# Eight of sixteen row blocks of x turned on VectorE, and the attention of quad 0 moved later, in a two-layer encoder step

## The chip, the cores and the metric

The kernel runs on one core of one Trainium2 chip. The metric is the device time of one execution in microseconds (us). It is an fp32 kernel: each product of the large projections is made of three fp32r matmuls on TensorE (PE). ACT and VectorE (DVE) split the weights, ACT and DVE also do the activations and the softmax, GpSimd (POOL) and SyncE (SP) mostly issue DMA transfers.

## The reference

One step of a two-layer encoder on 384 rows: 256 rows of a new stream ("prompt") and 8 running streams of 16 rows each ("sample"), with caches of 128 rows.

```python
DEPTH = 2; D_MODEL = 2048; SEQ = 256; DEC_BATCH = 8; DEC_SEQ = 16; PAST_LEN = 128
HEAD_DIM = 128; FOX_HEADS = 8; SB_HEADS = 8; C_WIDTH = 4096

def ab_project(h, w_in0, b_forget):
    p = jnp.einsum('bsd,dn->bsn', h, w_in0)        # q, k, v, gate of 8 + 8 heads, 8 forget logits
    ...

def fox_core(q, k, v, Fq, Fk, qpos, kpos):
    s = jnp.einsum('bqhd,bkhd->bhqk', q, k).astype(jnp.float32) * ATTN_SCALE
    s = s + (jnp.swapaxes(Fq, 1, 2)[..., :, None] - jnp.swapaxes(Fk, 1, 2)[..., None, :])
    s = jnp.where(kpos[None, :] <= qpos[:, None], s, -jnp.inf)
    p = jax.nn.softmax(s, axis=-1)
    return jnp.einsum('bhqk,bkhd->bqhd', p.astype(v.dtype), v)
```

Layer 0 is an RMSNorm, the projection above, forgetting attention (`fox_core`) for eight heads and stick-breaking attention for eight more, both gated, and an output projection with the residual added. Layer 1 is an RMSNorm, a projection to u, v and a gate, a spatial mix of the normalised v over 128 positions, and an output projection. A last RMSNorm follows. Outputs are the rows of both streams, and the new keys, values and forget logits.

## The kernel before

**Products.** A projection multiplies the 384 rows (three row tiles `tb` of 128) by 512 columns of a weight matrix, over 16 blocks `k` of 128 of the model's 2048 columns. The left operand is h, kept transposed as a high and a low half (`hhi`, `hlo`, tiles named `slot`). A weight tile of 128 rows by 512 columns comes over SP's queue (`raw`, five buffers). ACT casts it to its high half (`whi`, four buffers), DVE subtracts for its low half (`wlo`, four buffers), and `products` issues for two blocks at a time high x high (L100), high x low (L101) and low x high (L102): 18 matmuls of 128x512 for a pair of blocks. They are called products below. Their sums stand in a pool of four PSUM banks (`d`). All other matmuls share a second pool of four banks (`a`).

**Start.** The first projection (`first`, keys of heads 0 to 3) runs over the groups (0), (1), (2,3), ... (14,15) of blocks while x arrives in eight pieces of 256 columns over SP's queue (`load_piece`). For each block `x_transposes` turns three 128x128 tiles on TensorE (L219); ACT makes the high half of h out of PSUM, scaled by the norm's gain (L223, `slot<-a,gT`), and DVE the low half (L227). Group i+1's transposes and casts are issued between two parts of group i's products. The function `then` ties the instructions of an engine to the order in which they are written. After the last group the squares of x are summed for the norm (L271); the natural x in the `slot` tiles 94 to 97 is used for them too. The next projection (`values_first`: values of heads 0 to 3, in halves of 256 columns, with the forget logits) has weight tiles of 128x2x256 (L90).

**Quads.** After that, quads g of four heads each follow, g = 0 to 3, each with projections k, v, q and z (gate). The attention of a quad is done in two pairs of heads, and its steps are hooked into later projections: `at(g, what, kp, f)` calls f ahead of block pair kp of projection `what` of quad g. The steps of a pair are

- `scores`: the score matmuls of the new rows (L626, L627, L629) and of the cache (L632), softmax on DVE and ACT, and the writing of the weights to a DRAM tile `wd` over ACT's queue (L667). POOL then reads `wd` back in blocks of 32 by 32, four transfers `slot<-wd` (L492), so that DVE can turn them within the blocks.
- `attended`: two DVE transposes (L670) into the tiles `PT` of the two heads, the matmuls by the values (L678, L684 to L686) and by the cached values (L682), the gating on DVE, and the write of the result (`d<-gz`). The loads of the next heads' cached values follow (`vcache`, two buffers).
- `mix_split`, when both pairs are through: the gated result, read back over DRAM in blocks (`slot<-d`), is turned and split into halves for the output projection.

The order of an engine's instructions is set by a list scheduler that keeps the written order where `tc.issue_after` ties two instructions; each engine then runs its list in order and waits on semaphores.

**Norm gains.** `gains(1)` (L164, L165) turns the second norm's gains through one bank `a`. It stands ahead of the cumulative sums of the forget logits (L358 to L373), which take four banks.

Of the kernel before, what the change touches and what calls it, by code (L numbers as in the profile page):

```python
# [15 lines left out]
P = 128  # L16
# [16 lines left out]
def f32(ap):  # L33
    return ap.bitcast(F32)
# [3 lines left out]
def tile_hybrid_step(  # L38
# [27 lines left out]
    def bank():  # L66
        return psa.tile([P, 512], F32, tag="a", name=nm("a"))
# [36 lines left out]

    def dense_nat(w, k0, c0, his, los, nk=None, between=None, out=None, ks=None):


        nk = nk or len(his)
        out = out or [dbank() for _ in range(NT)]
        for kp in range(0, nk, 2) if ks is None else ks:  # L110
            behind = ()
            if between and kp in between:
                with tc.issue_after(splits[-1]), tc.issue_after(highs[-1]):
                    behind = between[kp]() or ()
            ws = [wunit(w[(k0 + k) * P:(k0 + k + 1) * P, c0:c0 + 512], 1, 512, behind=behind) for k in (kp, kp + 1)]
            products(out, his, los, ws, kp, range(NT), 0, nk - 1)
        return out
# [39 lines left out]
    with ExitStack() as l0:  # L157
# [29 lines left out]

        def load_raw():
            k = len(raws)
            raws.append(wload(w_in0[k * P:(k + 1) * P, 1024:1536], 1, 512))  # L190
# [24 lines left out]

        def x_transposes(k):
            b = bank()
            for tb in range(NT):
                then("PE", lambda: PE.transpose(b[:, tb * P:(tb + 1) * P], xs[k // 4][:, tb, k % 4 * P:k % 4 * P + P], ident))  # L219
            gcol = gT[:, k:k + 1]  # L220
            hi, lo = hhi[k // 4][:, k % 4, :], hlo[k // 4][:, k % 4, :]
            if k:
                high = then("ACT", lambda: S.activation(hi, b[:, :T], AF.Copy, scale=gcol))  # L223
            else:

                high = then("DVE", lambda: V.tensor_scalar(out=hi, in0=b[:, :T], scalar1=gcol, scalar2=None, op0=ALU.mult))
            return high, then("DVE", lambda: V.scalar_tensor_tensor(out=lo, in0=b[:, :T], scalar=gcol, in1=f32(hi), op0=ALU.mult, op1=ALU.subtract))  # L227
# [26 lines left out]
        for i, ks in enumerate(groups):  # L254
            then("PE", lambda: products(first, h0h, h0l, ws, ks[0], range(1), 0, KT - 1) if i else first_products(0))
            nxt = []
            if i + 1 < len(groups):
                if 1 <= i < 5:
                    load_piece(i + 3)
                while len(raws) < min(ks[-1] + 6, KT):  # L260
                    load_raw()
                nxt = [first_unit(k) for k in groups[i + 1]]
                done += [x_transposes(k) for k in groups[i + 1]]
# [79 lines left out]
        def forget(o):  # L343
# [12 lines left out]
            gains(1)  # L356
# [26 lines left out]
            V.tensor_copy(Fnat, b4[:, :24].rearrange("p (t h) -> p t h", h=8))  # L383
            nFT = lp.tile([8, 2 * T], F32, tag="PT", name="nFT")[:, :T]
# [81 lines left out]
        def quad(g):  # L466
# [11 lines left out]
            def scores(pair):  # L478
# [8 lines left out]
                for _ in range(2):  # L487
                    for j, hh in enumerate(pair):
                        own[hh].send(wd[j])
# [7 lines left out]
            def attended(pair):  # L497
                for j, hh in ((1, pair[1]), (0, pair[0])):
                    own[hh].send(own["blk", pair][:, j, :])
                for hh in pair:  # L500
                    next(own[hh])
# [9 lines left out]
            places = ((("z", 12), ("k", 2), ("k", 8), ("k", 12)), (("z", 12), ("v", 2), ("k", 2), ("k", 8)))[g > 0]  # L511
            at(g, "q", 2 if g == 0 else 14, lambda: turned("k"))
            at(g, "z", 12, lambda: turned("q"))
            for i, (what, kp) in enumerate(places):
                at(g + (what == "k"), what, kp, lambda i=i: (scores, attended)[i // 2](((0, 1), (2, 3))[i % 2]))
            at(g + 1, "q", (12, 8, 8, 8)[g], lambda: mix_split())
# [84 lines left out]
        def head(g, h, kT, values, qT, kc, vc, gate):  # L601
# [68 lines left out]
            V.transpose(out=PT, in_=blk)  # L670
            yield
# [320 lines left out]
```

## Time and profile before

| | us |
|---|---|
| three timed runs | 1812.33, 1812.5, 1813.67 (median 1812.5) |
| profiled execution, own time | 1815.39 |
| its span | 1813.7 |
| mean granted TensorE clock of the span | 0.995 |

The profile is one execution. Its span runs from the first to the last instruction, and the execution's own time lies 1.7 us above it. In a row of the timeline the two numbers ahead are the start and the length in us, `x8` counts instructions that follow one another, and the bracket holds the idle time of the engine just ahead and what ended it. Matmuls overlap, so that the distance from start to start is what one costs, not the length in its row. In a row of the windows stand busy time and count for PE, PEld (weight loads), DVE, ACT and POOL, then the granted clock, the share of the 16 DMA engines and GB/s. Names with a `q` (ACTq, POOLq, SPq) are the issues of DMA transfers on an engine's queue. The rows of ACT's largest wait read as follows.

```profile
ACT whi L84 <- PE d L102: 889.3, 379, 21.8
```

ACT waits 889.3 us in 379 places for TensorE to give back a `whi` buffer: the weight casts run ahead as far as four buffers let them, and TensorE paces them.

### The profile page before, as it was taken

To read this page: it belongs to the slowest core of one execution; us is meant where nothing else is said; L and a number is where in the kernel's file an instruction comes from. 1 tells how busy PE (TensorE), PEld (TensorE's weight loads), DVE (VectorE), ACT (ScalarE), POOL (GpSimd) and SP (SyncE) were. 2 spreads that over 40 slices of the span, in tenths; PEclk is the share of its full clock that TensorE was granted. 3 is DMA by queue.
4 is the path that set the end of the run, shared out by engine and by line. 5 is a ranking of instruction groups with operands and counts; after the bars stand their busy time and mean duration, and the time that the engine had idled before them with its cause. 6 is when DMAs were issued, how large, how long until landed. Compare 5 with 4: busy or idle time off the path is not lost. (4 is left out here: it accounts for less than half of the span.)

```text
span 1813.7 us, 24384 instructions
## 1 busy us (share of the span) xinstructions
PE 1788.8 (99%) x8575; PEld 1483.8 (82%) x8575; DVE 924.2 (51%) x1538; ACT 710.2 (39%) x1261; POOL 369.9 (20%) x544
## 2 busy tenths in 40 slices
PE   9999799999999999999999999999999999999998
PEld 8988588888888888888888888888888888888887
DVE  6337356458448455543433544554544563455366
ACT  5435236337337344433333333333333333333334
POOL 1515524313312202200300120320130210220020
PEclk9999899999999999999999999999999999999999
DMA  6868778878876877644444444454544554555553
GB/s 195 233 179 212 201 216 216 251 196 206 238 207 179 241 204 207 189 128 128 135 129 131 138 137 146 148 146 130 157 143 128 146 154 128 145 146 150 164 145 117
DMA packets 185771, 307.63 MB, mean 170 GB/s; under 512 B 22904, under 2 KB 63152, under 8 KB 185648
## 3 DMA queue, kind: packets, MB, share of 16 engines
q1 hardware_dynamic: 127696, 225.37, 42.1%
q0 software_dynamic: 25072, 63.53, 14.1%
q10 hardware_dynamic: 32880, 17.18, 3.2%
q8 instruction: 67, 1.10, 0.3%
q14 instruction: 56, 0.46, 0.1%
HBM read 269.23 MB, written 30.47 MB: 165 GB/s over the span
## 5 line engine op out<-in xcount | busy, mean ns | idle before, releaser
L86 DVE TENSOR_TENSOR wlo<-raw,whi 128x512 fp32r<-128x512 f32 x784 | 538.0, 695 | 745.1 <-ACT whi L84 744.9
L101 PE MATMUL d<-wlo,slot 128*128 128x512 f32 x2349 | 916.6, 391 | 0.2
L102 PE MATMUL d<-whi,slot 128*128 128x512 f32 x2349 | 912.0, 389 | 0.0
L84 ACT ACTIVATE whi<-raw 128x512 fp32r<-128x512 f32 x784 | 493.4, 631 | 944.9 <-PE d L102 889.3
L100 PE MATMUL d<-whi,slot 128*128 128x512 f32 x2349 | 822.9, 391 | 0.0
L100 PEld LDWEIGHTS d<-whi,slot 128*128 128x128 f32 x2349 | 440.9, 188 | 94.3 <-ACT whi L84 1.6
L101 PEld LDWEIGHTS d<-wlo,slot 128*128 128x128 f32 x2349 | 441.0, 188 | 91.7 <-DVE wlo L86 1.0
L102 PEld LDWEIGHTS d<-whi,slot 128*128 128x128 f32 x2349 | 441.0, 188 | 91.5
L126 POOL DMA_DIRECT2D gTt<-trn x128 | 78.0, 618 | 446.0 <-issue 263.9
L396 POOL DMA_DIRECT2D slot<-d x48 | 44.1, 924 | 145.9 <-DVE wlo L86 53.6
L492 POOL DMA_DIRECT2D slot<-wd x32 | 29.4, 924 | 103.4 <-DMA wd<-pr 34.6
L833 POOL DMA_DIRECT2D wr<-in_w_sp_dram x64 | 34.9, 553 | 26.2 <-DVE wT L837 25.1
L826 DVE TENSOR_TENSOR slot<-d,slot 128x512 f32<-128x512 f32 x48 | 32.0, 686 | 12.4 <-PE d L102 12.4
L783 POOL DMA_DIRECT2D slot<-in_sgu_ln_g_dram x8 | 4.5, 567 | 135.5 <-PE d L102 135.5
L455 POOL DMA_DIRECT2D kcache<-in_cache_sb_k_dram x32 | 24.9, 786 | 32.4 <-DVE KT L621 32.4
L455 POOL DMA_DIRECT2D kcache<-in_cache_fox_k_dram x32 | 25.0, 789 | 23.4 <-DVE KT L621 22.2
L709 POOL DMA_DIRECT2D blk<-h1d x12 | 11.0, 919 | 70.7 <-DMA h1d<-slot 60.4
L799 POOL DMA_DIRECT2D bcol<-in_b_sp_dram x1 | 1.2, 1176 | 116.1 <-DVE w L798 116.1
L862 PE MATMUL a<-vt,wT 128*128 128x256 f32 x96 | 24.5, 380 | 0.0
L777 POOL TENSOR_SCALAR rsv<-mvr 128x3 f32<-128x3 f32 x1 | 0.5, 540 | 113.0 <-DVE mvr L776 113.0
L774 DVE BATCH_NORM_STATS2 stats<-vt 128x6 f32<-128x512 f32 x24 | 16.3, 690 | 11.4 <-ACT vt L773 11.4
L849 DVE SCALAR_TENSOR_TENSOR gate<-d,rstd,gate 128x512 f32<-128x512 f32 x24 | 17.4, 748 | 7.3 <-PE d L102 7.3
(239 smaller groups left out, 1201.3 us busy)
## 6 DMA issues: line engine op xcount, KB each, us to landing
raw<-in_w_in_dram SPq DMA_DIRECT2D x640, 256.0 KB, 2.8
raw<-in_w_out_dram SPq DMA_DIRECT2D x189, 256.0 KB, 3.4
slot<-d POOLq DMA_DIRECT2D x48, 192.0 KB, 6.2
d<-slot ACTq DMA_DIRECT2D x24, 256.0 KB, 3.9
wd<-pr ACTq DMA_DIRECT2D x16, 384.0 KB, 5.8
slot<-wd POOLq DMA_DIRECT2D x32, 192.0 KB, 5.3
gTt<-trn POOLq DMA_DIRECT2D x128, 48.0 KB, 3.5
kcache<-in_cache_fox_k_dram POOLq DMA_DIRECT2D x32, 128.0 KB, 5.8
```

The costliest lines, as they stand in the source:

```text
L84: highs.append(S.activation(hi, raw, AF.Copy).ins)
L86: splits.append(V.tensor_tensor(out=lo, in0=raw, in1=f32(hi), op=ALU.subtract).ins)
L100: PE.matmul(o, lhsT=his[k][:, t], rhs=hi[:, 0, :], start=(k == first), stop=False)
L101: PE.matmul(o, lhsT=his[k][:, t], rhs=lo[:, 0, :], start=False, stop=False)
L102: mm = PE.matmul(o, lhsT=los[k][:, t], rhs=hi[:, 0, :], start=False, stop=(k == last))
L126: G.dma_start(dst[32 * j:32 * j + 32, :, 32 * a:32 * a + 32], trn[32 * a:32 * a + 32, :, 32 * j:32 * j + 32])
L396: r = G.dma_start(blk[32 * j:32 * j + 32].rearrange("p h (a d) -> p (h a) d", d=32), d[:, :, 32 * j:32 * j + 32].rearrange("h (a p) d -> p ...
L455: G.dma_start(k[32 * j:32 * j + 32].rearrange("p (b d) -> p b d", d=32), (c_fox_k, c_sb_k)[n // 8][:, :, n % 8, 32 * j:32 * j + 32].rearra ...
L492: G.dma_start(blk[32 * j:32 * j + 32].rearrange("p j (a d) -> p (j a) d", d=32), wd[:, :, :, 32 * j:32 * j + 32].rearrange("j x (a p) d -> ...
L826: evicted = V.tensor_tensor(out=h1[c][:, tb, :], in0=o[tb], in1=h1[c][:, tb, :], op=ALU.add)
L833: G.dma_start(wr[js, 0, :].rearrange("p (a s) -> p a s", s=32), w_sp[g, :, js].rearrange("(a p) s -> p a s", p=32))
L862: PE.matmul(m[:, i * 256:(i + 1) * 256], lhsT=wTs[i][:, tb // 2, :], rhs=vt[:, tb, cs], start=True, stop=True)
```

## The change

Four things are changed.

1. Blocks 8 to 15 of x are read from DRAM a second time, in blocks of 32 by 32 (`load_blocks`: 16 transfers for two blocks of x, of 32x8x32 or 32x4x32 elements, 64 in all, over POOL's, SP's and ACT's queues), into tiles `xblk` that use buffers which the attention needs later. `x_blocks` turns a pair on DVE with one instruction. The transposes of these blocks on TensorE go; ACT and DVE read the halves of h from the turned tile `xT` in SBUF. The natural x of these blocks (pieces 4 to 7) is still loaded for the squares, later.
2. `scores` issues the first score matmuls of its two heads behind the last product issued so far (`last_product`), then those of the cache, without products between. `attended` issues the matmuls of its two heads behind both DVE transposes.
3. In quad 0 the places move: the second `scores` stays, the first `attended` goes from (1,"k",8) to (1,"k",12), the second from (1,"k",12) to (1,"q",4), and `mix_split` from (1,"q",12) to (1,"z",4).
4. `gains(1)` stands behind the cumulative sums.

```diff
+    last_product = []
...
-            products(out, his, los, ws, kp, range(NT), 0, nk - 1)
+            last_product[:] = [products(out, his, los, ws, kp, range(NT), 0, nk - 1).ins]
...
+        xblk, FB = {}, 8
+
+        def load_blocks(k):
+
+            tag, shape = (("pr", [P, 2 * T]), ("kcache", [P, 8 * P]), ("vcache", [P, 8, P]))[(k - FB) // 2 % 3]
+            t = lp.tile(shape, F32, tag=tag, name=nm("xblk"))
...
+            V.tensor_copy(t[:, ::P], f32(h0h[k - FB][:, 0:6]))
+            for j in range(4):
+                for kk in range(2):
+                    cs = slice((k + kk) * P + 32 * j, (k + kk) * P + 32 * j + 32)
+                    o = t[32 * j:32 * j + 32, kk * T:kk * T + T].rearrange("p (a d) -> p a d", d=32)
+                    q = nc.sync if kk and j < 2 else G
+                    q.dma_start(o[:, :8], x_prompt[0, :, cs].rearrange("(a p) d -> p a d", p=32))
+                    q = nc.sync if kk else nc.scalar if k > FB else G
+                    q.dma_start(o[:, 8:], xview[2][:, cs].rearrange("(a p) d -> p a d", p=32))
...
+        def x_blocks(k):
+            b = lp.tile([P, 2 * T], F32, tag="PT", name=nm("xT"))
+            then("DVE", lambda: V.transpose(out=b, in_=xblk[k]))
+            xblk[k], xblk[k + 1] = b[:, :T], b[:, T:]
+
         def x_transposes(k):
-            b = bank()
-            for tb in range(NT):
-                then("PE", lambda: PE.transpose(b[:, tb * P:(tb + 1) * P], xs[k // 4][:, tb, k % 4 * P:k % 4 * P + P], ident))
+            if k < FB:
+                b = bank()
+                for tb in range(NT):
+                    then("PE", lambda: PE.transpose(b[:, tb * P:(tb + 1) * P], xs[k // 4][:, tb, k % 4 * P:k % 4 * P + P], ident))
+            else:
+                b = xblk[k]
...
-                if 1 <= i < 5:
-                    load_piece(i + 3)
+                if i in (1, 2, 3, 4):
+                    load_blocks(FB + 2 * i - 2)
+                if 4 <= i < 8:
+                    load_piece(i)
                 while len(raws) < min(ks[-1] + 6, KT):
                     load_raw()
+                if groups[i + 1][0] >= FB:
+                    x_blocks(groups[i + 1][0])
...
-            gains(1)
...
             V.tensor_copy(Fnat, b4[:, :24].rearrange("p (t h) -> p t h", h=8))
+            gains(1)
...
-                for _ in range(2):
-                    for j, hh in enumerate(pair):
-                        own[hh].send(wd[j])
+                with tc.issue_after(last_product[0]):
+                    for hh in pair:
+                        next(own[hh])
+                for j, hh in enumerate(pair):
+                    own[hh].send(wd[j])
...
             def attended(pair):
-                for j, hh in ((1, pair[1]), (0, pair[0])):
-                    own[hh].send(own["blk", pair][:, j, :])
-                for hh in pair:
-                    next(own[hh])
+                turned = [own[hh].send(own["blk", pair][:, j, :]) for j, hh in ((1, pair[1]), (0, pair[0]))]
+                with tc.issue_after(turned[0].ins), tc.issue_after(turned[1].ins):
+                    for hh in pair:
+                        next(own[hh])
...
-            places = ((("z", 12), ("k", 2), ("k", 8), ("k", 12)), (("z", 12), ("v", 2), ("k", 2), ("k", 8)))[g > 0]
+            places = (((0, "z", 12), (1, "k", 2), (1, "k", 12), (1, "q", 4)), ((0, "z", 12), (0, "v", 2), (1, "k", 2), (1, "k", 8)))[g > 0]
...
-            at(g + 1, "q", (12, 8, 8, 8)[g], lambda: mix_split())
+            at(g + 1, *(("z", 4) if g == 0 else ("q", 8)), lambda: mix_split())
...
-            V.transpose(out=PT, in_=blk)
-            yield
+            yield V.transpose(out=PT, in_=blk)
```

The order of instructions shows three places. The first is DVE's list around the transposes of quad 0's second pair of heads, before the change; `wlo` are the low halves of the weights of quad 1's projections, two for each pair of blocks.

```order
L86 TENSOR_TENSOR wlo_2164<-raw_2160,whi_2162 128x512
L86 TENSOR_TENSOR wlo_2170<-raw_2166,whi_2168 128x512
L86 TENSOR_TENSOR wlo_2194<-raw_2190,whi_2192 128x512
L86 TENSOR_TENSOR wlo_2200<-raw_2196,whi_2198 128x512
L670 STREAM_TRANSPOSE PT_2029<-slot_1816 128x768
L670 STREAM_TRANSPOSE PT_2031<-slot_1816 128x768
```

With the change the same two transposes (line 706 of the changed file) stand among the casts of the projection q, behind those of its blocks 0 to 3:

```order
L86 TENSOR_TENSOR wlo_2302<-raw_2298,whi_2300 128x512
L86 TENSOR_TENSOR wlo_2308<-raw_2304,whi_2306 128x512
L86 TENSOR_TENSOR wlo_2332<-raw_2328,whi_2330 128x512
L86 TENSOR_TENSOR wlo_2338<-raw_2334,whi_2336 128x512
L706 STREAM_TRANSPOSE PT_2215<-slot_1864 128x768
L706 STREAM_TRANSPOSE PT_2217<-slot_1864 128x768
```

The matmuls of this pair have moved with them: 732 products are ahead of it before, counted from the start of the program, and 808 with the change, 76 more. Those of the first pair stand behind 678 and 690 products (its two heads apart) before, and together behind 684 with the change.

The second place is ACT's list at the end of the first projection, before the change: the weight casts of blocks 12 to 15 (`whi_389` to `whi_431`), the casts of x blocks 12 to 15 out of the banks `a` into h's high half (`slot_135`), and the squares.

```order
L231 ACTIVATE whi_389<-raw_305 128x512
L231 ACTIVATE whi_393<-raw_345 128x512
L223 ACTIVATE slot_135<-a_397,gT 128x384
L223 ACTIVATE slot_135<-a_403,gT 128x384
L231 ACTIVATE whi_427<-raw_347 128x512
L231 ACTIVATE whi_431<-raw_387 128x512
L223 ACTIVATE slot_135<-a_435,gT 128x384
L223 ACTIVATE slot_135<-a_441,gT 128x384
L271 ACTIVATE sq_477,ssq<-slot_94 128x512
```

With the change, where `xT` is the tile turned on DVE:

```order
L261 ACTIVATE whi_449<-raw_371 128x512
L261 ACTIVATE whi_453<-raw_407 128x512
L253 ACTIVATE slot_135<-xT_447,gT 128x384 x2
L261 ACTIVATE whi_483<-raw_409 128x512
L261 ACTIVATE whi_487<-raw_445 128x512
L90 ACTIVATE whi_665<-raw_663 128x2x256
L90 ACTIVATE whi_691<-raw_689 128x2x256
L253 ACTIVATE slot_135<-xT_481,gT 128x384 x2
L305 ACTIVATE sq_525,ssq<-slot_94 128x512
```

Two weight casts of the next projection (L90) now stand ahead of the casts of x blocks 14 and 15.

The third place is SP's list of transfers at the start, with the change; `xblk_177` and `xblk_229` are x blocks 8 to 11 in 32 by 32 blocks.

```order
L74 DMA raw_156<-in_w_in_dram 128x512
L206 DMA xblk_177<-in_x_prompt_dram 32x8x32
L208 DMA xblk_177<-in_x_sample_dram 32x4x32
L206 DMA xblk_177<-in_x_prompt_dram 32x8x32
L208 DMA xblk_177<-in_x_sample_dram 32x4x32 x3
L74 DMA raw_195<-in_w_in_dram 128x512
L206 DMA xblk_229<-in_x_prompt_dram 32x8x32
L208 DMA xblk_229<-in_x_sample_dram 32x4x32
L206 DMA xblk_229<-in_x_prompt_dram 32x8x32
L208 DMA xblk_229<-in_x_sample_dram 32x4x32 x3
```

Between two weight tiles stand six transfers of x blocks here; before the change stood two of natural x.

More of the change, by code (lines that the diff above doesn't have):

```diff
@@ L186, in load_piece @@
             load_x(xs[i // 2][:, :, c0:c0 + n], i // 2 * 512 + c0, n, q)
+        xblk, FB = {}, 8
+        def load_blocks(k):
+            tag, shape = (("pr", [P, 2 * T]), ("kcache", [P, 8 * P]), ("vcache", [P, 8, P]))[(k - FB) // 2 % 3]
+            t = lp.tile(shape, F32, tag=tag, name=nm("xblk"))
+            if len(shape) == 3:
+                t = t.rearrange("p b d -> p (b d)")
+            xblk[k] = t = t[:, :2 * T]
+            V.tensor_copy(t[:, ::P], f32(h0h[k - FB][:, 0:6]))
[7 more added lines that the diff above has]
+                    q.dma_start(o[:, 8:], xview[2][:, cs].rearrange("(a p) d -> p a d", p=32))
         def load_raw():
@@ L508, in attended @@
                     mixed.append(blocks(own["d"])[0])
-            places = ((("z", 12), ("k", 2), ("k", 8), ("k", 12)), (("z", 12), ("v", 2), ("k", 2), ("k", 8)))[g > 0]
+            places = (((0, "z", 12), (1, "k", 2), (1, "k", 12), (1, "q", 4)), ((0, "z", 12), (0, "v", 2), (1, "k", 2), (1, "k", 8)))[g > 0]
             at(g, "q", 2 if g == 0 else 14, lambda: turned("k"))
             at(g, "z", 12, lambda: turned("q"))
-            for i, (what, kp) in enumerate(places):
-                at(g + (what == "k"), what, kp, lambda i=i: (scores, attended)[i // 2](((0, 1), (2, 3))[i % 2]))
-            at(g + 1, "q", (12, 8, 8, 8)[g], lambda: mix_split())
+            for i, (later, what, kp) in enumerate(places):
+                at(g + later, what, kp, lambda i=i: (scores, attended)[i // 2](((0, 1), (2, 3))[i % 2]))
+            at(g + 1, *(("z", 4) if g == 0 else ("q", 8)), lambda: mix_split())
             def evict(o, dst, scale, n=512):
```

## The prediction, made before the changed kernel was run

> **What bounds the kernel now.** I read the page's busy times first, then TensorE's waits, then the timeline around the longest one.
>
> ```profile
> span 1813.7 us, 24384 instructions
> PE 1788.8 (99%) x8575; PEld 1483.8 (82%) x8575; DVE 924.2 (51%) x1538; ACT 710.2 (39%) x1261; POOL 369.9 (20%) x544
> ```
>
> TensorE is busy 99% of the span, and 24.9 us are left. What can be won is idle time of TensorE, time at a low clock, and matmuls that go away; what the other engines save is worth nothing by itself.
>
> ```profile
> PE a L678 <- DVE PT L670: 13.5, 1, 13.5
> PE a L373 <- DVE gT L165: 1.3, 1, 1.3
> ```
>
> These are the two waits of TensorE (total, times, longest) that the change touches. The larger one is a single event: the first value matmul of quad 0's second pair of heads waits for the transposed weights PT. The columns of the next fence are start, length, engine, line; the first three rows are that event, the last three the same work of a later quad that waits for nothing.
>
> ```profile
> 195.63 0.39 PE L102 MATMUL d<-whi,slot 128*128 128x512 f32 x1
> 209.53 0.65 PE L678 MATMUL a<-vnat,PT 128*32 128x128 f32 x8 [13.51 <-DVE PT L670]
> 214.32 0.48 PE L100 MATMUL d<-whi,slot 128*128 128x512 f32 x1
> ...
> 334.81 0.39 PE L102 MATMUL d<-whi,slot 128*128 128x512 f32 x1
> 335.12 0.42 PE L678 MATMUL a<-vnat,PT 128*32 128x128 f32 x8
> 337.93 0.47 PE L100 MATMUL d<-whi,slot 128*128 128x512 f32 x1
> ```
>
> From product to product that is 214.32 - 195.63 = 18.69 us against 337.93 - 334.81 = 3.12, so the event costs 15.57 us. The wait explains 13.5; the rest is the clock, as the windows show (PE busy, ..., granted clock, DMA share, GB/s):
>
> ```profile
> 200.00:205.00 5.00, 0.00 (x0) 0.00 (x0) 0.00 (x0) 0.00 (x0) 4.53 (x5) 0.51 0.67 184
> 205.00:210.00 5.00, 0.47 (x12) 0.43 (x16) 1.84 (x2) 0.00 (x0) 1.87 (x4) 0.50 0.26 58
> 210.00:215.00 5.00, 5.00 (x59) 4.40 (x52) 1.06 (x5) 0.00 (x0) 1.81 (x2) 0.62 0.38 111
> ```
>
> The granted clock falls to 0.5 while TensorE stands still and is only 0.62 on average when the small matmuls run. The Trainium skill, "TensorE: Matmul & The Clock Gate", Part 1, says that the clock halves after an idle window of about 3.4 us and comes back after as long a busy one; the trace agrees (0.51, then 0.62). By that rule a remainder under 3.4 us would cost its own length only, a longer one some 2 us more.
>
> **The chain behind the wait.**
>
> ```profile
> 185.53 0.38 ACTq L667 DMA_DIRECT2D wd<-pr  x1
> 200.46 3.70 POOL L492 DMA_DIRECT2D slot<-wd  x4 [9.53 <-DMA wd<-pr]
> 207.64 1.84 DVE L670 STREAM_TRANSPOSE PT<-slot 128x768 f32<-128x768 f32 x2 [12.41 <-DMA slot<-wd]
> DMA to landing us min/median/max: 3.5/5.3/14.2
> ```
>
> The weights go to DRAM (issued at 185.53, landed by 200: this is the 14.2 of the last row, which groups wd's transfers), come back in 32 by 32 blocks (issued 200.46 to 204.16, landed about 207.6) and are turned in 1.84 us, done at 209.48.
>
> **Part by part.**
>
> *Second pair of quad 0 moved to (1,"q",4).* By the instruction order it now stands 76 products later. The pitch of products, over ten of them:
>
> ```profile
> 11.71 0.40 PE L101 MATMUL d<-wlo,slot 128*128 128x512 f32 x1
> ...
> 13.99 0.39 PE L102 MATMUL d<-whi,slot 128*128 128x512 f32 x1
> ```
>
> 0.228 us each, so TensorE arrives 17.3 us later, at about 195.86 + 17.3 - 0.3 = 212.9 in the clock of before; PT was ready at 209.5. The 15.57 us go if the chain doesn't move by more than 3.4 us. It moves a little: the first pair's transposes stand behind two more weight casts on DVE, which puts wd's issue about 1 us back, and TensorE no longer pauses, so that weights (256 KB per 2.7 us) keep flowing while wd is written and read back. With all of it PT would be ready between 210 and 213.5, or later. I put a rest of 0.5 us, bounds 0 and 5 (5: wd 1 us later and a read-back of twice its 7 us, less the slack of 3.4). What is late next is mix_split's transposed read of quad 0, moved from (1,"q",12) to (1,"z",4) with it: the gated values land some 20 us after the matmuls, about 233, and are wanted at about 235; I put nothing, 2 at worst.
>
> *First pair merged.* Before, its heads are two groups; merged, one.
>
> ```profile
> 180.01 0.39 PE L101 MATMUL d<-wlo,slot 128*128 128x512 f32 x1
> 182.12 0.39 PE L101 MATMUL d<-wlo,slot 128*128 128x512 f32 x1
> ...
> 338.25 0.39 PE L101 MATMUL d<-wlo,slot 128*128 128x512 f32 x1
> ```
>
> One group: 182.12 - 180.01 = 2.11, less two products (0.455), 1.655. A merged one: 338.25 - 334.81 = 3.44 less 0.455, 2.985. Two of the first less one of the second: -0.33 us.
>
> *Scores merged, four second pairs.* Each loses one return to the products; bounds 0 and 4 x 0.33 = 1.3. The groups are shorter by only a few hundredths each where a split and a merged one can be compared, so I take -0.2.
>
> *x of blocks 8 to 15 through DVE.* Four groups of six transposes leave TensorE.
>
> ```profile
> 14.22 0.82 PE L219 MATMUL a<-ident,slot 128*128 128x128 f32 x6
> 15.11 0.40 PE L101 MATMUL d<-wlo,slot 128*128 128x512 f32 x1
> ```
>
> From the product at 13.99 to the second one behind, 15.11 - 13.99 = 1.12, less two products, 0.66 each: -2.7 us for four. DVE takes on four transposes of 128x768 (0.92 each, as in the row at 207.64) and has room: it is busy 2.7 of 5 us there.
>
> *The price at the start: DMA.* 64 transfers of 16 or 32 KB in pieces of 128 bytes, 1.5 MB, come on top; the natural x is still read for the squares.
>
> ```profile
> 5.00:10.00 5.00, 4.79 (x17) 3.91 (x18) 3.04 (x6) 2.48 (x5) 0.36 (x2) 1.00 1.04 364
> 10.00:15.00 5.00, 5.00 (x30) 4.25 (x29) 3.64 (x7) 2.86 (x6) 0.00 (x0) 1.00 1.07 377
> 15.00:20.00 5.00, 5.00 (x27) 4.15 (x26) 2.52 (x4) 2.53 (x5) 0.00 (x0) 1.00 0.94 317
> 20.00:25.00 5.00, 5.00 (x27) 4.14 (x26) 2.57 (x5) 2.53 (x6) 0.00 (x0) 1.00 0.38 117
> 25.00:30.00 5.00, 5.00 (x27) 4.14 (x26) 2.72 (x5) 2.52 (x5) 0.00 (x0) 1.00 0.38 118
> 30.00:35.00 5.00, 5.00 (x27) 4.15 (x26) 2.88 (x6) 2.50 (x5) 1.34 (x1) 1.00 0.50 93
> ...
> q0 software_dynamic: 25072, 63.53, 14.1%
> q10 hardware_dynamic: 32880, 17.18, 3.2%
> ```
>
> The engines now work 5 x (1.04 + 1.07 + 0.94 + 0.38 + 0.38 + 0.50) = 21.5 of these 30 us. The nearest transfers in 128-byte pieces are POOL's own (slot<-wd, 192 KB each), on queue q0: 14.1% of 1813.7 us x 16 engines for 63.53 MB is 15.5 bytes per ns and engine, so 1.57 MB more take all 16 engines 6.3 us: 27.8 of 30, just fitting. The other end is q10's 3.2%, 28 ns per packet, if each of the 12288 pieces takes as long as such a packet: 21.5 us, 43 of 30, and TensorE starves. The Trainium skill, "DMA: Bandwidth & Descriptors", § Why small descriptors are slow, speaks against this part: a fixed 3 cycles per piece beside 4 beats of 32 bytes; by that the extra would be an estimated 9 us and not 6.3, 1 us past the room. The 15.5 against some 18 bytes per ns of q10's longer packets agrees with it in sign, not in size. Besides, SP issues six of each block's transfers ahead of a weight tile at about 0.45 us each, so that tiles 7 to 11 are asked for up to 5 us later, and a tile needs about 3 to land; I find their slack at 0 to 1 us. I take +1 us, bounds 0 and 4.
>
> *A new wait at the end of the first projection.* On ACT two casts of the following projection's weights (whi, 128x2x256) now stand ahead of the casts of x blocks 14 and 15. whi has four buffers, all held by the last two groups, so the second of them waits for group (12,13)'s last matmul, and the x casts behind it for as long. Group (14,15)'s first matmul waits for those. The prices, TensorE first:
>
> ```profile
> 35.90 0.40 PE L102 MATMUL d<-whi,slot 128*128 128x512 f32 x1
> ...
> 36.34 1.32 ACT L231 ACTIVATE whi<-raw 128x512 fp32r<-128x512 f32 x2 [1.36 <-PE d L102]
> 38.71 1.05 ACT L223 ACTIVATE slot<-a,gT 128x384 fp32r<-128x384 f32 x2 [1.06 <-PE a L219]
> ```
>
> From the start of the releasing matmul to the cast 0.44, the cast 0.53 to 0.66, the x cast 0.52 to 0.58, and some 0.3 for the low half on DVE behind it, whose second product comes a pitch later: 2.0 less the 0.23 until TensorE could have gone on anyway. +1.8 us, bounds 0 and 2.5.
>
> *gains(1) later.* It held one of four PSUM buffers that the cumulative sums need.
>
> ```profile
> 73.32 1.03 PE L373 MATMUL a<-sums,clf 128*8 128x128 f32 x8
> 75.69 1.05 PE L373 MATMUL a<-sums,clf 128*8 128x128 f32 x8 [1.33 <-DVE gT L165]
> ```
>
> Eight at (1.03 - 0.27) / 7 = 0.109 take 0.87 of the 2.37 between the starts: -1.5 us. The buffers are four for four tiles then; nothing else stands in the way. The eight matmuls behind this wait take 1.05 us, as the eight ahead of it: a wait of this length leaves the clock alone, and so should the 1.8 above.
>
> **Sum**, against the profiled execution's 1815.4 us: -15.6 + 0.5 - 0.3 - 0.2 - 2.7 + 1.0 + 1.8 - 1.5 = -17.0, or 1798.4. The three timed runs have a median of 1812.5, 2.9 less; the same change on it gives **1795.5 us**.
>
> **The rivals.**
>
> *The read-back is late again.* If wd's write and read take as much longer as TensorE runs on (the transfers between 185 and 200 ran at a share over 0.9), PT comes at 216 to 218: 3 to 5 us of wait and up to 2 of low clock, 1799 to 1802. For it: the 14.2 us landing is the longest of sixteen and the traffic behind it no less. Against it: 3.4 us of slack. 0.15.
>
> *The start is starved.* The pieces' bad end: late weights cost 4 to 10 us, 1799 to 1806. For it: a share of 1.0 already in the first 15 us; against it: the 15.5 bytes per ns. 0.15.
>
> *Nothing is lost at the start* and the casts' wait hides: without the three added terms 1792.2, or somewhat under. 0.15.
>
> *Slower.* The same pieces as a mechanism that goes further: at 28 ns a piece the demand of 43 us in 30 starves TensorE for 13, with low clock perhaps 17, and the change comes out even. Above some 33 ns (25 us of demand for the pieces, 16 beyond the room, with cold clocks 20 or more) it is slower: at 40 ns 1820. POOL's own rows speak against it; the hardware queues' 128-byte pieces, 0.7 MB of the 1.5, are shown by no row. 0.03.
>
> *The change doesn't do what it says*, because the 13.5 us wait is an accident of one execution: then 1812.5 - 1.4 = 1811. The three runs lie within 1.3 us, and the chain is made of fixed places; 0.02.
>
> **How the numbers follow.** The forecast gets 0.5, with 1793.5 to 1798.5 as its own range. The range for 8 in 10 takes in the gain without added costs and most of the two late cases: 1790.5 to 1803.5. 0.2% is 3.6 us, about what a measurement here can tell from no change. Everything up to 1808.9 is faster: the forecast and the first three rivals but for 0.02 of their tails, 0.93; within it those tails and the wait that was an accident, 0.04; slower 0.03.
>
> **What would show it.** TensorE's waits have no 13.5 us row, or one under 2; the clock at 200 to 215 is 1.0. No transposes L219 for blocks 8 to 15; the first projection's end about 1 us earlier than before if +2.8 is right, 2.7 earlier if nothing is added. A wait of some 1.8 us for an x cast ahead of group (14,15). No wait on gT. Wrong it would be if TensorE waited for whi or raw between 15 and 35 us by more than 4, or for PT again by more than 3.

## The result, and the profile after

| | before | after |
|---|---|---|
| median of six runs, us | 1813.09 (1812.2 to 1813.8) | 1803.34 (1802.38 to 1805.93) |
| ratio after to before, 95% | | 0.9948 [0.9935, 0.9961] |
| profiled execution, us | 1815.39 | 1802.38 |
| its span, us | 1813.7 | 1800.6 |

The change makes the kernel faster by 0.52%, 9.75 us between the medians. Forecast were 17.0 us. The direction and the place of the gain came out as forecast; the size is little over half.

The page of the changed kernel:

```profile
span 1800.6 us, 24453 instructions
PE 1785.0 (99%) x8551; PEld 1478.7 (82%) x8551; DVE 928.5 (52%) x1546; ACT 709.8 (39%) x1261; POOL 385.7 (21%) x572
```

TensorE's waits (total, times, longest) in the changed kernel:

```profile
PE d L100 <- ACT slot L253: 5.7, 3, 3.0
```

The 13.5 us for PT and the 1.3 us for gT are gone. In their place TensorE waits three times for ACT's cast of h (L253 of the changed file, L223 before). The windows show where that is (busy time and count of PE, PEld, DVE, ACT, POOL, granted clock, DMA share, GB/s):

```profile
25.00:30.00 5.00, 3.46 (x14) 2.21 (x14) 2.86 (x5) 2.16 (x4) 1.71 (x3) 1.00 0.74 175
30.00:35.00 5.00, 2.35 (x11) 1.60 (x9) 0.58 (x2) 0.89 (x2) 0.00 (x0) 1.00 0.96 285
...
200.00:205.00 5.00, 5.00 (x24) 4.14 (x23) 2.71 (x3) 2.14 (x4) 4.99 (x6) 1.00 1.09 305
205.00:210.00 5.00, 5.00 (x24) 4.14 (x23) 2.07 (x3) 1.32 (x3) 5.00 (x7) 1.00 1.04 189
```

Where TensorE stood still at a clock of 0.5 before, at 200 to 210, it is now busy throughout at 1.00. At 25 to 35, where it was busy throughout before, 4.2 of 10 us are idle. The timeline of TensorE around the three waits (start, length, engine, line):

```profile
25.75 0.39 PE L102 MATMUL d<-whi,slot 128*128 128x512 f32 x1
27.66 0.50 PE L100 MATMUL d<-whi,slot 128*128 128x512 f32 x1 [1.53 <-ACT slot L253]
...
31.96 0.39 PE L102 MATMUL d<-whi,slot 128*128 128x512 f32 x1
35.30 0.50 PE L100 MATMUL d<-whi,slot 128*128 128x512 f32 x1 [2.95 <-ACT slot L253]
...
43.67 0.39 PE L102 MATMUL d<-whi,slot 128*128 128x512 f32 x1
45.28 0.50 PE L100 MATMUL d<-whi,slot 128*128 128x512 f32 x1 [1.23 <-ACT slot L253]
```

Less a pitch of 0.23 each, they cost 1.68, 3.11 and 1.38 us, 6.2 together; behind each the next products come later by some 0.4 us more. ACT's own timeline shows what the cast of h stood behind each time:

```profile
23.31 2.52 ACTq L208 DMA_DIRECT2D xblk<-in_x_sample_dram  x4
26.48 0.63 ACT L261 ACTIVATE whi<-raw 128x512 fp32r<-128x512 f32 x1 [4.15 <-DMA xblk<-in_x_sample_dram]
27.01 1.11 ACT L253 ACTIVATE slot<-xT,gT 128x384 fp32r<-128x384 f32 x2
...
34.11 0.63 ACT L261 ACTIVATE whi<-raw 128x512 fp32r<-128x512 f32 x1 [5.47 <-DMA raw<-in_w_in_dram]
...
43.41 1.31 ACT L90 ACTIVATE whi<-raw 128x512 fp32r<-128x512 f32 x2 [2.39 <-PE d L102]
44.63 1.11 ACT L253 ACTIVATE slot<-xT,gT 128x384 fp32r<-128x384 f32 x2
```

The first time ACT itself issues four transfers of x blocks until 25.8, since they wait for earlier transfers to land, and then it still waits for a weight tile, asked for at 23.06 and landed at 26.37 by the trace's semaphores; the second time another weight tile lands late, at 34.01; the third time it is the wait forecast, for a `whi` buffer. The late tile of the second time stands on SP behind six transfers of x blocks and two of natural x:

```profile
24.54 0.33 SPq L206 DMA_DIRECT2D xblk<-in_x_prompt_dram  x1
25.19 0.33 SPq L208 DMA_DIRECT2D xblk<-in_x_sample_dram  x1
26.39 0.31 SPq L206 DMA_DIRECT2D xblk<-in_x_prompt_dram  x1
26.74 1.78 SPq L208 DMA_DIRECT2D xblk<-in_x_sample_dram  x3
28.57 0.43 SPq L154 DMA_DIRECT2D slot<-in_x_prompt_dram  x1
29.04 0.47 SPq L155 DMA_DIRECT2D slot<-in_x_sample_dram  x1
29.61 0.85 SPq L74 DMA_DIRECT2D raw<-in_w_in_dram  x2
```

The six issues take from 24.5 to 28.5, since several wait for the landing of an earlier transfer (the one at 26.39 for the weight tile that lands at 26.37), and the tile asked for at 29.6 is cast at 34.1. Counting products in the two traces gives the balance. F is the time from the first product of block 1 (10.13 before, 8.81 after) to the first of the last three of the first projection (45.01 and 49.11). Without transposes of blocks 8 to 15 it should have lost 2.7; it went from 34.88 to 40.30:

| stretch, by counted products | before | after |
|---|---|---|
| program start to block 1 | 10.13 | 8.81 |
| F, the first projection | 34.88 | 40.30 |
| N, from there to the first 128x512 product behind the values' projection | 40.76 | 39.66 |
| product 500 to 680, with quad 0's second pair | 62.79 | 47.19 |

### The profile page after: what moved, and what is told of

It reads as the page before. It is cut to its first block, busy times and chain, and to the rows that moved or that the text cites. A ratio compares the mean times of both kernels' runs of the same rounds, so it can differ in the third digit from the quotient of the medians.

```text
span 1800.6 us, 24453 instructions
## 1 busy us (share of the span) xinstructions
PE 1785.0 (99%) x8551; PEld 1478.7 (82%) x8551; DVE 928.5 (52%) x1546; ACT 709.8 (39%) x1261; POOL 385.7 (21%) x572
## 5 line engine op out<-in xcount | busy, mean ns | idle before, releaser
L86 DVE TENSOR_TENSOR wlo<-raw,whi 128x512 fp32r<-128x512 f32 x784 | 540.0, 697 | 742.1 <-ACT whi L84 741.6
L91 DVE TENSOR_TENSOR wlo<-raw,whi 128x512 fp32r<-128x512 f32 x16 | 11.0, 691 | 20.0 <-ACT whi L90 20.0
```

The costliest lines, as they stand in the source:

```text
L86: splits.append(V.tensor_tensor(out=lo, in0=raw, in1=f32(hi), op=ALU.subtract).ins)
```

## The experiments

The theory (Q) after this reading: the pair's place gives all of the gain; the x blocks lose 5 us because weight tiles and casts stand behind their issues. Rivals: V, the wait of 13.5 us varies and is worth less in other executions; X, the x blocks gain and the loss lies elsewhere; P, it isn't the queues but the DMA engines' time on pieces of 128 bytes. The medians are of four to six executions, but e1 is a single one; an interval of the ratio is some 2.4 us to either side. F and N are counted in one trace each.

| run | median, us | ratio to before, 95% | F | N | F + N |
|---|---|---|---|---|---|
| before | 1813.09 to 1813.85 | 1 | 34.88 | 40.76 | 75.64 |
| changed kernel | 1803.34 | 0.9948 [0.9935, 0.9961] | 40.30 | 39.66 | 79.96 |
| e1 before again | 1813.06 | | 34.87 | 39.28 | 74.15 |
| e2 no x blocks | 1798.45 | 0.9913 [0.9900, 0.9926] | 34.89 | 39.16 | 74.05 |
| e3 only x blocks | 1819.25 | 1.0031 [1.0019, 1.0043] | 41.46 | 41.28 | 82.74 |
| e10 only places | 1797.70 | 0.9914 [0.9900, 0.9927] | 34.92 | 40.60 | 75.52 |
| e7 casts later | 1802.21 | 0.9936 [0.9923, 0.9949] | 39.42 | 39.12 | 78.54 |
| e4 long pieces | 1802.69 | 0.9939 [0.9927, 0.9951] | 36.71 | 39.12 | 75.83 |
| e8 weights first | 1799.48 | 0.9923 [0.9912, 0.9935] | 35.82 | 40.64 | 76.46 |
| e12 ACT free | 1800.15 | 0.9923 [0.9911, 0.9936] | 36.56 | 40.58 | 77.14 |
| e6 weights first, ACT free | 1799.60 | 0.9923 [0.9911, 0.9936] | 35.05 | 40.61 | 75.66 |
| e9 long pieces, weights first | 1799.22 | 0.9918 [0.9905, 0.9932] | 35.01 | 40.59 | 75.60 |
| e11 all three | 1797.70 | 0.9907 [0.9894, 0.9919] | 32.69 | 40.60 | 73.29 |
| e5 four blocks, on POOL | 1796.54 | 0.9905 [0.9893, 0.9918] | 33.50 | 39.16 | 72.66 |

**e1, the kernel before once more.** Nothing is edited.

> The kernel before, a second profile. Theory Q (the pair's wait is fixed by its places; what is lost is lost at the start): the wait of L678 for PT is 13.5 us within 1 again, the clock behind it 0.5, and the execution takes about 1813, the 2 us by which the first profiled execution was longer lying at the program's start or spread thin. Rival V (the wait varies from execution to execution): a wait of 10 to 12 us, the difference sitting there.

TensorE's wait in that execution, and behind it two of its windows:

```profile
PE a L678 <- DVE PT L670: 13.9, 1, 13.9
```

```profile
200.00:205.00 5.00, 0.00 (x0) 0.00 (x0) 0.00 (x0) 0.00 (x0) 4.57 (x7) 0.50 0.63 152
205.00:210.00 5.00, 2.58 (x48) 2.17 (x48) 1.84 (x2) 0.00 (x0) 0.73 (x1) 0.50 0.08 18
```

The wait is there again, as long, with the clock at 0.5: V falls. (In e3, where the x blocks come ahead of it, it is 12.0.) This execution was 2.3 us shorter than the one of the first profile; its block 1 starts at 8.68 in place of 10.13, and N is 39.28 in place of 40.76, without any wait for gT.

**e2, the change without x blocks.**

```diff
-        xblk, FB = {}, 8
+        xblk, FB = {}, KT
...
-                if i in (1, 2, 3, 4):
-                    load_blocks(FB + 2 * i - 2)
-                if 4 <= i < 8:
-                    load_piece(i)
+                if 1 <= i < 5:
+                    load_piece(i + 3)
```

> The change without its first part: x of all blocks is turned on TensorE, the other three parts stay. Theory Q: the first projection ends as it did before the change, 5.4 us earlier than in the changed kernel; the whole is before less 15.6 (pair) less 1.1 (gains) less 0.5 (merges), a ratio of 0.990 to 0.991 (about 1796), and 5 to 7 us under the changed kernel. Rival V: 0.992 to 0.994, since the pair's move is worth less than its profile said. Rival X (the x blocks gain and the loss lies elsewhere): no faster than the changed kernel, 1803 to 1806.

1798.45, a ratio of 0.9913, a little above the 0.991 expected: the x blocks of the change cost 0.35% (0.9948 - 0.9913; 4.9 us between the medians), and F is back at 34.89.

**e3, x blocks alone.** The part on x blocks is put into the kernel before, nothing else.

> Only the first part on the kernel before: x blocks 8 to 15 through DVE. Theory Q: slower by 5.4 us (4 to 7), a ratio of 1.002 to 1.004, with TensorE waiting for the casts of h three times between 20 and 46 us. Rival X: 0.9985 to 1.0005, as the prediction had it for this part (-2.7 + 1.0 + 1.8 = +0.1).

1.0031: slower by 0.3%, as Q has it, and X falls. In its trace some 1.6 us of F are lost to half clock behind one of the waits (see the last section). Its waits of TensorE:

```profile
PE a L710 <- DVE PT L702: 12.0, 1, 12.0
PE d L100 <- ACT slot L251: 4.7, 4, 2.0
PE a L405 <- DVE gT L165: 1.9, 1, 1.9
```

The pair's wait stays (here on lines 702 and 710), and four waits for casts of h come on top.

**e10, the places alone**, in the kernel before: the table of places and the hook of `mix_split` from the change, with the matmuls of two heads and the gains as they were.

```diff
+            places = (((0, "z", 12), (1, "k", 2), (1, "k", 12), (1, "q", 4)), ((0, "z", 12), (0, "v", 2), (1, "k", 2), (1, "k", 8)))[g > 0]
...
+            at(g + 1, *(("z", 4) if g == 0 else ("q", 8)), lambda: mix_split())
```

> The kernel before with the new places of quad 0 alone: second pair of heads at (1,q,4), first at (1,k,12), mix_split at (1,z,4). If the pair's place is the whole gain: 15.6 less, a ratio of 0.9910 to 0.9918 (1797 to 1799), no wait of L678 over 1 us, granted clock 1.0 there. If the merging of the two heads' matmuls or the order of the norm gains is needed for it: 1800 or more.

```profile
PE a L373 <- DVE gT L165: 1.2, 1, 1.2
```

No wait for PT is left, and the ratio is 0.9914, 15.6 of 1813: within the interval the gain of the whole change without x blocks (e2). The new places are the gain; what merging and the order of the norm gains bring is smaller than the intervals.

The other runs take the x blocks' loss apart.

**e4, long pieces.** The x blocks' transfers read rows of 1024 and 512 bytes.

```diff
-                    q.dma_start(o[:, :8], x_prompt[0, :, cs].rearrange("(a p) d -> p a d", p=32))
+                    q.dma_start(o[:, :8].rearrange("p a d -> p (a d)"), x_prompt[0, 32 * j:32 * j + 32, k * P - 2 * j * 32:k * P - 2 * j * 32 + 256])
...
-                    q.dma_start(o[:, 8:], xview[2][:, cs].rearrange("(a p) d -> p a d", p=32))
+                    q.dma_start(o[:, 8:].rearrange("p a d -> p (a d)"), xview[2][32 * j:32 * j + 32, (k + kk) * P:(k + kk) * P + P])
```

> The changed kernel with the same 64 transfers of the same bytes on the same queues, but read in contiguous pieces of 1024 and 512 bytes in place of 128; so x blocks 8 to 15 hold other columns of x, and the output is not the reference's. Theory Q (the weights and casts stand behind the issues on SP and ACT, which wait for landings): at least 3 of the 5.4 us stay, 1801 to 1804. Rival P (the 128-byte pieces take the DMA engines' time): 4 us or more go, 1797 to 1799.

The time hardly moves, 0.9939, as Q expects; but the scheduler also placed the casts of the next projection later in this kernel, as in e7, so that e7 is its partner. F is 2.7 us below e7's in the traces, but some 1.4 of that are lost to half clock in e7's trace, which this one has not; the median is 0.5 above e7's. This trace loses 2 us behind N, with a wait of 0.6 for PT and one of 0.9 for a `whi`. The transfers' use of the 16 engines between 10 and 30 us, in e7 and then in e4 (packets, MB, share):

```profile
q1 hardware_dynamic: 5447, 2.47, 50.1%
q0 software_dynamic: 895, 0.85, 19.9%
q10 hardware_dynamic: 1728, 0.20, 7.1%
```

```profile
q1 hardware_dynamic: 2402, 2.48, 41.4%
q0 software_dynamic: 896, 0.85, 18.1%
q10 hardware_dynamic: 576, 0.20, 3.9%
```

The same bytes take 77.1% of the engines with short pieces and 63.4% with long ones: the pieces cost 13.7% of 20 us, 2.7 us of all engines, though the engines have room. This alone doesn't show in the median.

**e7, the casts later.** The first two casts of the values' projection wait for the last casts of h.

```diff
-                split(hi[:, :, :256], lo[:, :, :256], raw)
+                with late() if forget and u < 2 else ExitStack():
+                    split(hi[:, :, :256], lo[:, :, :256], raw)
```

> The changed kernel with the next projection's first two weight casts tied behind the casts of x blocks 14 and 15 on ACT and DVE; nothing else. If this order is what makes TensorE wait before group (14,15): the wait of 1.4 there goes, the time falls by 1 to 2 us (1801.5 to 1802.5), and the two earlier waits stay. It is also the kernel that the one with long pieces is to be compared with, which has the same order on ACT: pieces that matter (theory P) make this one 2 us or more slower in the first projection than that, issues alone (theory Q) leave both alike within 1.

1802.21 against 1803.34, 0.9936 against 0.9948, in the direction and size expected, though the intervals overlap. In the trace the stretch from product 117 to 141, with the last group's start, falls from 7.26 to 5.44 us (5.47 before the change). But a wait of 1.97 us ahead of 29.53 is followed by half clock here, which costs some 1.4 us, so that F falls by 0.9 alone; and F of the runs below is to be compared with 38.0 rather than 39.42.

**e8, weights first.** Only the order on SP.

```diff
+                while len(raws) < min(ks[-1] + 6, KT):
+                    load_raw()
                 if i in (1, 2, 3, 4):
                     load_blocks(FB + 2 * i - 2)
                 if 4 <= i < 8:
                     load_piece(i)
-                while len(raws) < min(ks[-1] + 6, KT):
-                    load_raw()
```

> The changed kernel with SP's order alone turned: a group's weight tiles ahead of its x blocks (the scheduler then places the casts later by itself). Theory Q: the 3 us wait for the weights goes, the one behind ACT's issues stays, 1.5 to 2 us: 1799 to 1800.5. Theory P: no more than the casts' order brings, 1801 to 1802.5.

1799.48, within what Q expects, and F 35.82, 3.6 us below e7's or 2.2 without e7's half clock. The wait of 3 us is gone, the first one is 0.5, and a new one of 1.3 stands at 38.17. The place in SP's queue is a part of the loss, with the pieces as short as before, though the intervals of the two runs overlap. N is 1.5 longer than e7's: TensorE waits 0.9 us for the low halves of the values' weights.

**e12, ACT free of transfers**, its twelve moved to POOL, SP's order as in the change, the casts later.

```diff
-                    q = nc.sync if kk else nc.scalar if k > FB else G
+                    q = nc.sync if kk else G
```

> The changed kernel with the casts later and the 12 transfers on ACT moved to POOL; pieces of 128 bytes and SP's order as in the change. Against the run that has the casts later alone (first projection 39.4 us, 1802.2): if ACT's issues are a large part, 36 to 37.5 us and 1799.5 to 1801; if the weights behind the x blocks on SP set the pace by themselves, 39 to 40 us and 1801.5 to 1803.

1800.15 and F 36.56, both as expected if ACT's issues are a large part. The traces don't bear this out: of 2.9 us below e7's F 1.4 are e7's half clock, and N is 1.5 longer, with a wait of 1.1 us for a low half of the values' weights. This run leaves the part of ACT's issues open; e9 and e11 tell more.

**e6, weights first and ACT free**, both edits and the casts later.

> All eight x blocks through DVE in the same 64 transfers, but SP asks for the weight tiles of a group ahead of its x blocks, and the 12 transfers on ACT go to POOL; casts later. Theory Q: the waits of the first projection go but for 1 us, and what is left is the gain of four groups of transposes: 1796 to 1798. Theory P: at least 2 us of waits stay, 1799 to 1801.

1799.60, F 35.05: the two don't add up. Over the 32.2 (34.88 less 2.7) of a first projection without waits 2.9 us remain, and 1.4 more in N, so the expectation of Q (1796 to 1798) is missed and P's (1799 to 1801) met.

**e9, long pieces and weights first.**

> Long pieces (as in the run with long pieces: x blocks 8 to 15 hold other columns, so the output is not the reference's), the weight tiles ahead of the x blocks on SP, and the casts later, all at once. If length of the pieces and place in SP's queue are two parts of one delay (weight tiles that land too late), together they leave nothing of it: the first projection from its first pair of blocks on takes 32.2 to 33.2 us (34.9 before less 2.7), the time is 1795 to 1797. If a third thing holds the weights (ACT's own issues), 34 to 36 us and 1798 to 1800.

1799.22, F 35.01: the second case, a third thing still holds TensorE back.

**e11, all three at once.**

> The run before with long pieces and the weight tiles first, and now the 12 transfers on ACT go to POOL as well (x blocks 8 to 15 hold other columns, so the output is not the reference's). If ACT's own issues, between its casts, are what was left: the first projection from its first pair of blocks on takes 32.2 to 33.2 us, the time is 1795.5 to 1797.5. If not ACT but the late natural x or the late weights behind 24 transfers on SP: 34 to 36 us and 1798 to 1800.

F 32.69, within the 32.2 to 33.2 expected, but 1797.70 is just past the time expected. In F nothing of the loss is left; N, however, is 40.60, 1.4 more than in e2:

```profile
PE a L460 <- DVE wlo L91: 1.2, 1, 1.2
```

```profile
37.72 0.98 DVE L240 STREAM_TRANSPOSE xT<-xblk 128x768 f32<-128x768 f32 x1 [2.18 <-DMA xblk<-in_x_prompt_dram]
```

The last x blocks are turned at 37.7, and the squares and the low halves of the values' weights stand behind them on DVE, so that a part of the loss has moved into the next projection. F + N is 73.29, where e2 less four groups of transposes would be 71.4: of the 2.7 us of the transposes 0.8 are won, as the medians have it (1797.70 against 1798.45). Against e9, which has ACT's issues, F is 2.3 us less and the median 1.5; against e6, which has the short pieces, 2.4 and 1.9. The intervals overlap both times, so that the sizes rest on one trace each: ACT's issues, and the pieces' length where the queues are cleared, some 2 us each.

**e5, four blocks on POOL.** x blocks 12 to 15 alone, all 32 transfers on POOL's queue, the casts later.

```diff
-        xblk, FB = {}, 8
+        xblk, FB = {}, 12
...
-                if i in (1, 2, 3, 4):
+                if i in (1, 2):
                     load_blocks(FB + 2 * i - 2)
-                if 4 <= i < 8:
-                    load_piece(i)
+                if i in (1, 2, 5, 6):
+                    load_piece(i + 3 if i < 5 else i + 1)
...
-                    q = nc.sync if kk and j < 2 else G
+                    q = G
...
-                    q = nc.sync if kk else nc.scalar if k > FB else G
+                    q = G
```

> Only x blocks 12 to 15 through DVE, their 32 transfers all on POOL's queue, SP and ACT free of them; the casts later as in the run before. Theory Q: the first projection takes its time before less two groups of transposes (1.3), so 1 to 2 us under the kernel without x blocks, 1796.5 to 1797.5. Theory P: half of the pieces' time is left, and the kernel stays at or above the one without x blocks, 1798 to 1800.

```profile
PE a L218 <- DVE ones L134: 1.1, 1, 1.1
PE a L247 <- DMA slot<-in_x_sample_dram: 0.2, 1, 0.2
```

Both waits stand ahead of block 1. No wait of the first projection behind it is left, F is 33.50, which is 34.88 less two groups of transposes to within 0.1, N is as short as in e2, and 1796.54 is the fastest of the kernels here that compute the reference's output: 0.9905 of before. These 32 transfers do no harm on a queue behind which nothing waits. They are half as many as in the change; all 64 on POOL's queue were not run.

## Why the prediction was right in its direction and wrong in its size

*The second pair of quad 0* was forecast at -15.6 + 0.5. By the stretch from product 500 to 680 it brought -15.6 and no rest (with the old places the stretch takes 63.38 in e1 and 61.12 in e3, so that 13.9 to 16.2 are gained). The chain behind it:

```profile
189.62 0.37 ACTq L703 DMA_DIRECT2D wd<-pr  x1
...
199.54 3.69 POOL L528 DMA_DIRECT2D slot<-wd  x4 [6.34 <-DMA raw<-in_w_in_dram]
...
211.79 1.84 DVE L706 STREAM_TRANSPOSE PT<-slot 128x768 f32<-128x768 f32 x2 [1.92 <-DMA slot<-wd]
...
216.10 0.42 PE L713 MATMUL a<-vnat,PT 128*32 128x128 f32 x8
```

PT is ready at 213.63 and TensorE comes at 216.1: 2.5 us of slack (3.4 by the forecast, less what it let the chain slip). The total is right, the parts are not: from the write's issue to the read 9.9 us pass (14.9 before), from the read to the transposes 12.3 (7.2 before). The read-back was late by 5 us, as the rival "read-back late again" has it, and a write shorter by 5 us made up for it; that no rest is left is luck in part. In e4 the slack is used up, and TensorE waits 0.6 us for PT. The wait of `mix_split` did not come.

*The price at the start* is the step that failed. It was written "I take +1 us, bounds 0 and 4". From F, 40.30 - 34.88 + 2.7 for the transposes make 8.1 us of loss: the 6.2 of the three waits, and some 0.4 behind each of them and at 21.4, where the products of a group also begin late. Less the 1.4 of the casts' wait and some 0.4 behind it, 6.3 us are the price, past the upper bound. The forecast looked at the engines' room (27.8 of 30 us) and at SP's issues as 0.45 us each. What it left out is that issues wait: six issues took 4 us, because transfers wait for the landing of earlier ones, and the weights and ACT's casts wait behind them in their queues. The semaphores in the traces show which earlier ones: the transfers of SP and ACT take turns on eight semaphores, and an issue waits until the transfer that had its semaphore before has landed, a weight tile or an x block alike; POOL's transfers have eight of their own. Between 5 and 37 us SP and ACT issue 28 transfers before the change and 60 with it. At 3.8 us from issue to landing (the median of the x blocks) 60 transfers, eight at a time, take an estimated 28.5 of these 32 us. In the trace 31 of the 55 issues between 8 and 37 us leave within 0.1 us of such a landing, before the change 4 of 21. The rival "the start is starved" named late weights at 4 to 10 us, but for the engines' lack of time and with a chance of 0.15. By e8, e9 and e11 the order on SP, the issues on ACT and the length of the pieces each take part; only with all three mended is F without loss.

The Trainium skill, "DMA: Bandwidth & Descriptors", § Why small descriptors are slow, was the better guide to the pieces themselves: from its fixed cost of each packet the prediction had an estimate of 9 us of all engines for the 1.57 MB. In the changed kernel the queues of POOL and ACT took 20.9% and 7.5% of 16 engines in the 20 us from 10 to 30 (packets, MB, share):

```profile
q0 software_dynamic: 896, 0.85, 20.9%
q10 hardware_dynamic: 1728, 0.20, 7.5%
```

On ACT's queue that is 14 ns a packet, 8 to 9 bytes per ns and engine, where POOL's 15.5 had been taken for all. POOL's own queue moves its part in 896 packets of some 950 bytes, at 12.7 bytes per ns: its rows were not of packets of 128 bytes. With SP's 0.52 MB at ACT's rate the 64 transfers take an estimated 9.6 us of all engines. The 33 ns from which the change would have been slower were far off.

*The casts' wait* of (14,15) was forecast at 1.8, bounds 0 and 2.5; the wait itself cost 1.38, with the late products behind it 1.8 (7.26 less 5.47 in the stretch of e7's trace above), and e7, without it, 1.1 us less in the median. This term was right.

*The transposes*, -2.7: e5's F gives 0.69 per group, and e11's F all four to within 0.5.

*gains(1)*, -1.5: the wait was read from one execution. e1 runs the same order without it, e3 and e10 have it with 1.9 and 1.2. In the change N is 1.1 less than in the first profile and 0.4 more than in e1. Of the four traces with the old order N is 40.76, 39.28, 41.28 and 40.60, against 39.16 in e2, so the term is 1.3 on average and 0.1 to 2.1 in one execution. What it is worth in the median is not shown: the ratios of e2 and e10, without it and with it, agree, but their intervals are wider than the term.

*The first pair merged*, -0.33: not gained. The two heads' matmuls stand together, but the scheduler mixed them, and the group costs what the two did:

```profile
184.31 0.39 PE L102 MATMUL d<-whi,slot 128*128 128x512 f32 x1
...
188.09 0.40 PE L101 MATMUL d<-wlo,slot 128*128 128x512 f32 x1
```

3.78 less two products, 3.32, against 2 x 1.655 before.

*The scores*, -0.2: some 0.06 in quad 0 (86.76 to 86.70 from the values' projection to product 500) and 0.3 behind product 680.

*The execution*: the sum was made against 1815.4, an execution 2.3 us above the later runs' median. The traces' balance is -13.1 in the spans, 1.3 of it at the program's start, where the change does nothing: e1 starts as early as the changed kernel. The other 11.8 are the forecast's 17.0 less 5.3, by which the price at the start was too small, to within 0.1; the errors of the other terms cancel.

## What to carry to other kernels

A place is moved by the slack of the whole chain behind it; the row of the wait with the clock in the windows gave that gain within 0.1 us in the trace that it was read from, and within 1.7 in others. For added transfers the engines' room is the smaller question: ask first what stands behind them on each queue that issues them, whether an issue can wait for a landing, and how many transfers can be under way at once. When a wait is taken away, look where it went: e11 lost its waits in one projection and got one in the next. A term read from a single wait of one to two microseconds in one execution should be looked for in a second profile.

## What was not expected of the hardware

A wait of 2 us lowered the clock twice, and one of 3 us did not. In e3 and in e7 TensorE waits 1.97 us, before 28.88 and 29.53, and a microsecond later the clock is at half for 3.41 us. The waits of 2.95 in the changed kernel, of 2.15 in e4 and of 1.97 in e12 leave it at 1.00. The traces show what decides. Half clock begins on a grid of 3.413 us that runs through the execution: in e3 at 29.80 and at 203.88, 51 steps apart, in the kernel before at 200.11 and at 1807.79, 471 steps apart. It lasts whole steps, one in e3 and e7 and four, 13.65 us, at the pair's wait. Windows cut on this grid in e3, in e7 and in the changed kernel (there reckoned back from the half clock at the program's end, at 1795.29):

```profile
26.39:29.80 3.41, 1.43 (x6) 0.57 (x5) 1.45 (x3) 2.11 (x4) 0.38 (x1) 1.00 0.78 188
29.80:33.21 3.41, 3.41 (x9) 2.67 (x10) 1.77 (x3) 0.06 (x1) 0.00 (x0) 0.50 0.72 191
```

```profile
26.49:29.90 3.41, 1.44 (x7) 0.86 (x5) 0.89 (x2) 1.55 (x4) 0.90 (x2) 1.00 0.87 221
29.90:33.31 3.41, 3.41 (x9) 2.45 (x8) 2.32 (x4) 0.61 (x2) 0.00 (x0) 0.50 0.58 150
```

```profile
30.60:34.01 3.41, 1.75 (x8) 1.13 (x6) 0.00 (x0) 0.00 (x0) 0.00 (x0) 1.00 0.92 265
34.01:37.42 3.41, 2.10 (x8) 1.45 (x9) 2.27 (x5) 2.80 (x5) 0.41 (x1) 1.00 1.04 359
```

In e3 and e7 the whole wait falls into one step; TensorE is busy for 1.4 of 3.4 us in it, and the next step runs at half. In the changed kernel the longer wait lies across two steps, busy for 1.75 and 2.10. In the fourteen traces each whole step at full clock with 1.45 us of busy TensorE or less is followed by one at half, and none with 1.75 or more; nothing lies between. The grid lies differently in each execution, so that the same wait can cost its own length in one and some 1.5 us more in the next. The changed kernel's profiled execution has a mean granted clock of 0.999, its other five have 0.997 or 0.998; whether their waits lowered the clock, no trace shows. The Trainium skill, "TensorE: Matmul & The Clock Gate", Part 1, sets the limit at an idle window of about 3.4 us; the length of the window agrees with the traces, but the window needn't be idle, as e3 and e7 show with 1.4 us busy. The prediction's sentence that waits of 1.3 to 1.8 us leave the clock alone holds for the rows it was read from.

The program's start takes two lengths, whatever the kernel: block 1's first product comes at 8.6 to 8.9 us in seven of fourteen traces and at 10.1 to 11.0 in the other seven, the kernel before among both (10.13 and 8.68).
